# A hybrid decoder block on one core: pads that put TensorE's operands at multiples of 512 bytes, one weight cast behind q's evictions, and other filler amounts around the attention values

## The chip, the cores and the metric

The kernel runs on one core of one Trainium2 chip. The metric is the device time of one execution in microseconds (us); several runs give a median. The profile is of one further execution. Engines are named as in the profile: PE is TensorE's matmul, PEld its weight load, DVE is VectorE, ACT is ScalarE, POOL is GpSimd, and SP is the queue from which most DMAs are issued.

## The reference

One decoder layer for 512 tokens of width 1024, in float32.

```python
h = rmsnorm(x, g_mix)
q_r,k_r,v_r,g_r, q_f,k_f,v_f,f_f, a_r,a_f = split(h @ w_in)
y_r = (silu(g_r) * groupnorm(retention(rot(q_r), rot(k_r), v_r))) @ w_ret_o   # 4 heads
y_f = forgetting_attention(rmsnorm(q_f), rmsnorm(k_f), v_f, log_sigmoid(f_f + b)) @ w_fox_o   # 8 heads of 64
x = x + (sigmoid(a_r) * y_r + sigmoid(a_f) * y_f) @ w_out
h2 = rmsnorm(x, g_ffn)
x = x + (silu(h2 @ w_gate) * (h2 @ w_up)) @ w_down                             # inner width 2816
```

Forgetting attention is causal softmax attention whose scores get the difference of two cumulated log forget gates added.

## The kernel before, in words

**Products.** Every float32 operand is split into a high and a low part (`wh`, `wl` for weights, `xh`, `xl`, `orh`, `orl`, `ofh`, `ofl`, `mgh`, `mgl`, `xfh`, `xfl` for activations, `hl` for both halves of the hidden activations and `ps` for both parts of the feed-forward weights). A product is three matmuls (`three`: high by high, low by high, high by low) into one PSUM bank. Most matmuls stream 512 columns of float32 against 128 x 128 stationary values. A weight unit of 128 x 1024 goes through four steps: a DMA on SP's queue into `raw` (`load_w`, through `move`, L69), ACT's cast into `wh` and DVE's difference into `wl` (`split_raw`, L160), and PE's matmuls. A unit takes a `raw` buffer (2) and a `wh`/`wl` buffer (3), so loads run ahead of PE by a few units.

**Order of the work.** After a start of some 5 us PE runs: the first token products (to about 66 us), q of the attention branch in two cuts of 256 and 264 columns (66 to 97 us), k and v (to 149 us), and then the gates. All of these are generators in one `Fill` (L281): `fill(x)` advances it by x us of PE work as the code reckons it (3 matmuls of 512 columns count 0.64, L28). Between the fills stand the steps of retention and of the attention ("fox"). So the amounts handed to `fill` set the order on PE. `pinned` keeps PE's, and `moves` SP's, instructions in the order in which the code issues them.

**q.** `tok_group` (L257) runs the cuts one after another; a cut uses four PSUM banks, one for each 128 tokens, and the second cut begins in the banks of the first, when `evac_qf` (L643) has copied them out with ACT. q has four weight units: 0 and 1 for the first cut, 2 and 3 for the second.

**Attention.** The loop (L947 to L972) makes 32 score steps: 4 pairs of heads `a`, 2 heads `e` in a pair, 4 query blocks `i`. A step makes two matmuls, then DVE's minimum and ACT's exponential; two steps later DVE transposes `pr` into `psq`. The transposed probabilities of a head are turned across partitions through DRAM: `fox_put` (L757) writes `psq` to `pd`, `fox_get` (L772) reads it back as `pT` in four DMAs that wait until the write has landed. Both go through SP's queue, in the order of the code, with the loads of weights (`raw`), forget-gate rows (`cb`) and row scales (`rd`, `rw`) between them. Pair `a`'s values (`fox_values`, L784; 16 matmuls `pT,vf`, called V0 to V3 here) stand at step 8(a+2)+1, behind `fill(VF)`. After a score step `fill(SF[i])` runs, where i counts down 3, 2, 1, 0; behind the last score steps `fill(TAIL)`.

**The stages after that.** The gate products and y_r (`orh`) to 285 us, W_fo (`ofh`) to 310 us, W_out (`mgh`, `mgl`) to 354 us, the feed-forward's gate and up products (`gu`, `ps,xfh`) to 568 us, and the down product (`hl,ps`) from 569 us. The parts `ps` go round a ring of three buffers r0, r1, r2, where r2 lies in the pool `fq`; `hl` lies in three other places, one of them (`b2f`) in `fq` too.

**Addresses.** [...] Three pads fill up what small tiles leave: `PAD_CST` (L108) ahead of the weight pool, `PAD_SM` (L109) on the right side, `PAD_FTOK` (L919) in the token pool. Distances of the first byte from the last multiple of 512, in the built program:

| tiles that PE reads | before |
|---|---|
| wh, wl, later mgh, mgl, and the pool fq (r2, b2f) | 32 |
| xh, xl, orh, orl, ofh, ofl, xfh, xfl, the ring's r0 and r1, the other two places of hl | 192 |
| retention's and the attention's working tiles | 448 |

So a product `xh,wh` streams or holds an operand that begins 32 bytes past a multiple of 64 and another that begins on a multiple of 64; `mgh,wh` has both at 32, and `ps,xfh` has both at 192, or one at 32 where ps is in r2.

Of the kernel before, what the change touches and what calls it, by code (L numbers as in the profile page):

```python
# [13 lines left out]
AF = mybir.ActivationFunctionType  # L14
# [13 lines left out]
MM3 = 3 / 2400.0  # L28
WARM = 8 * (512,) + 3 * (128,)
NEG = -1e30  # L30
PAD_CST, PAD_FTOK, PAD_SM = 107, 104, 16

C_GMIX = 0
C_GFFN = C_GMIX + NK
# [17 lines left out]
def block_kernel(ctx: ExitStack, tc, x, xT, c_early, c_tab, c_late, w_qf, w_tok, w_vg, w_a, w_y, w_o, w_gu, w_gl, w_dn, w_dh, out):  # L52
# [3 lines left out]
    act = nc.scalar.activation  # L56
    pinned = [False, None]

    def after(ins, prev):

        tc.add_manual_dep(ins.ins, prev.ins.name, mybir.DependencyInfo(mybir.DependencyClass.NoSync, mybir.DependencyReason.DATA), reason="order")
# [38 lines left out]
    def bank(tag):  # L100
        return ps.tile([P, 512], F32, name=tag, tag=tag, bufs={"acc": 4, "sc": 2, "tp": 2}[tag])
# [39 lines left out]

    WU, WP = 1056, 1152
    RAW, WB, SG, PT, CBUF, LEAD = 2, 3, 16, 2, 3, 2
    RF, CF, PF, SF, LAG = (5.72, 4.64, 6.8, 4.2, 11.2, 4.4), (3.0, 2.0, 2.26, 4.0), 5.9, (0.63, 0.83, 1.57, 1.4), 2
    VF, TAIL = 1.8, 2.6

    raw_pools, part_pools, turns = [wp] * RAW, [wp] * WB, [0, 0]

# [19 lines left out]
    def split_w(src, width=1024):  # L168
        h, l = ready.pop(0) if ready else split_raw(begun.pop(0) if begun else load_w(src, width), width)
        due[0] = LEAD  # L170
        return h, l
# [9 lines left out]
    def three(o, sh, sl, mh, ml, first, last):  # L181
        due[0] -= 1
        if due[0] == 0 and coming:
            begun.append(load_w(*coming.pop(0)))
        mm(o, lhsT=sh, rhs=mh, start=first, stop=False)
        mm(o, lhsT=sh, rhs=ml, start=False, stop=False)
        mm(o, lhsT=sl, rhs=mh, start=False, stop=last)
# [14 lines left out]
    for k in range(NK):  # L202
        u, cs = k // 2, slice(k % 2 * 512, k % 2 * 512 + 512)
# [53 lines left out]
    def tok_group(src, evac, cuts=(512,), done=(), behind=None):  # L257

        u = 0
        for c, w in enumerate(cuts):  # L260
            accs = [bank("acc") for _ in range(NT)]
            kpu = 1024 // (w // 256 * 256)
            for k in range(NK):
                if k % kpu == 0:
                    h, l = done[u] if u < len(done) else split_w(src(u, w * kpu), w * kpu)
                    if behind is not None and u == len(done):
                        after(split_raw.last[0], behind)
                    u += 1
                cs = slice(k % kpu * w, k % kpu * w + w)
                for t in range(NT):  # L270
                    tq = slice(t * P, (t + 1) * P)
                    three(accs[t][:, :w], xh[:, k, tq], xl[:, k, tq], h[:, cs], l[:, cs], k == 0, k == NK - 1)
                    if k == NK - 1:
                        evac(t, c, accs[t])
                    yield w * MM3
# [226 lines left out]
    fox = {}  # L502
# [107 lines left out]
    qf = ftok.tile([P, NT, FH * FD], F32, name="qf", tag="qf")  # L610
# [31 lines left out]

    def evac_qf(t, c, acc):  # L643
        sc = rstd1[:, t:t + 1]
        act(out=qf[:, t, c * 256:c * 256 + 256], in_=acc[:, 0:256], func=AF.Copy, scale=sc)  # L645
        if c:
            fox["fz"] = stt(out=fz[:, t, :], in0=acc[:, 256:264], scalar=sc, in1=ce[:, C_BF:C_BF + FH], op0=ALU.mult, op1=ALU.add)
            if t == NT - 1:
                for u in range(NT):
                    qnorm(u)  # L650
# [188 lines left out]
    def y_ret(mp):  # L839

        def evac(m2, acc):
# [4 lines left out]

    pinned[0] = True
    fill = Fill(tok_group(lambda u, width: w_qf[u, :, :width], evac_qf, (256, 264), (queue_q,), turn_act[0]),
                tok_group(unit(1), evac_kf), tok_group(unit(0), evac_to(vf, AF.Copy)), gates(0), gates(1), gates(2), gates(3), *(y_ret(mp) for mp in range(4)))
    coming += [(w_qf[u, :, :w * 4], w * 4) for u, w in ((1, 256), (2, 264), (3, 264))] + [(w_tok[g, u], 1024) for g in (1, 0) for u in range(4)]  # L850
    coming += [(w_a[g, mp, u], 1024) for mp in range(4) for g in range(2) for u in range(2)] + [(w_y[g, mp], 1024) for g in range(2) for mp in range(4)]
# [569 lines left out]
    def u_tile():  # L1421
        turns_u[0] += 1
        return u2[:, turns_u[0] % 2]

    turns_u = [0]
    for g in range(4):
# [12 lines left out]
        u = u_tile()  # L1439
# [131 lines left out]
```

## Time and profile before

| | |
|---|---|
| median of 3 runs | 692.83 us (692.82 to 693.55) |
| the profiled execution | 692.4 us, of it 690.6 span |
| PE busy | 682.4 us (99%), 3375 matmuls |
| PEld busy | 562.3 us (81%) |
| DVE busy | 536.1 us (78%) |
| ACT busy | 362.3 us (52%) |
| POOL busy | 53.5 us (8%) |
| DMA | 100.51 MB, mean 146 GB/s |
| granted TensorE clock | 1.000 |
| chain that ended last | PE 64%, DMA 3%, DVE 1%, ACT 1% |

The span runs from the first to the last instruction; the 1.8 us around it are in the time of an execution and not in the profile. The times of a row are a start, a duration, an engine, a line, an operation and the tiles `out<-in`, with a count; a bracket holds the idle time ahead of it and what ended that. A matmul's duration overlaps with that of the next, so PE's pace is read from the distance of starts and not from durations.

### The profile page before, as it was taken

The numbers are of one execution on the slowest core, as the hardware profiler recorded it, in microseconds if no ns is written. First come the engines' busy times: TensorE is split into PE (matmuls) and PEld (weight loads), VectorE is DVE, ScalarE is ACT, GpSimd is POOL, SyncE is SP. The second block draws the span as 40 slices with busy tenths as digits, with TensorE's granted clock in tenths as the row PEclk, the third lists the DMA queues.
The fourth block names the chain that finished last, engine by engine and source line by source line (L and its number), as shares of the span: only waits on it lengthen the run. The fifth ranks groups of instructions, "written<-read, shape, count | busy, mean of one in ns | idle before, by whom it ended". The sixth has DMA issues, their size and how long they took to land.

```text
span 690.6 us, 9419 instructions
## 1 busy us (share of the span) xinstructions
PE 682.4 (99%) x3375; PEld 562.3 (81%) x3375; DVE 536.1 (78%) x878; ACT 362.3 (52%) x551; POOL 53.5 (8%) x73
## 2 busy tenths in 40 slices
PE   9999999999999999999999999999999999999998
PEld 6887988887787768788888888888888898888997
DVE  6899458966688655496988898989889887756794
ACT  6777354642455435354576655564646474443341
POOL 0033600000122210000130000000000000000000
PEclk9999999999999999999999999999999999999999
DMA  8900543624648878527611516545362523654221
GB/s 290 398 7 31 134 158 93 214 92 153 198 136 264 235 193 247 166 92 263 224 62 45 200 30 166 136 140 154 86 177 59 143 72 62 158 144 156 80 103 62
DMA packets 85806, 100.51 MB, mean 146 GB/s; under 512 B 52960, under 2 KB 62464, under 8 KB 84992
## 3 DMA queue, kind: packets, MB, share of 16 engines
q1 hardware_dynamic: 84976, 98.86, 46.3%
q10 hardware_dynamic: 784, 1.07, 0.6%
q8 instruction: 26, 0.43, 0.3%
q14 instruction: 20, 0.16, 0.1%
HBM read 82.50 MB, written 10.58 MB: 135 GB/s over the span
## 4 chain that ended last, share of the span: by engine, by line
PE 64%; DMA 3%; DVE 1%; ACT 1%; SPq 0%; issue 0%; DVEq 0%; ACTq 0%
PE acc L81 49%; PE sc L81 11%; PE tp L81 4%; DMA pT<-pd 1%; DMA pd<-psq 1%; DMA tk<-tk 1%; SPq L71 0%; ACT ps L1073 0%; DVE ps L1074 0%; DVE b L1082 0%; ACT us L1236 0%; DVE us L1286 0%; DVE hl L1130 0%; DVE us L1235 0%; DVE pf L1460 0%
## 5 line engine op out<-in xcount | busy, mean ns | idle before, releaser
L81 PE MATMUL acc<-ps,xfh 128*128 128x512 f32 (+1 forms) x576 | 168.3, 374 | 0.3 <-ACT us L1195 0.3
L81 PEld LDWEIGHTS acc<-ps,xfh 128*128 128x128 f32 x576 | 105.3, 188 | 21.0 <-ACT us L1195 0.5
L1073 ACT CAST ps<-b 128x1024 fp32r<-128x1024 f32 (+1 forms) x84 | 82.2, 979 | 61.3 <-PE acc L81 27.4
L1074 DVE TENSOR_TENSOR ps<-b,ps 128x1024 fp32r<-128x1024 f32 (+1 forms) x84 | 94.4, 1135 | 22.2 <-ACT ps L1073 21.0
L81 PE MATMUL acc<-ps,xfl 128*128 128x512 f32 (+1 forms) x288 | 107.9, 375 | 0.0
L164 ACT CAST wh<-raw 128x1024 fp32r<-128x1024 f32 (+1 forms) x44 | 46.0, 1048 | 90.9 <-PE acc L81 50.5
L165 DVE TENSOR_TENSOR wl<-raw,wh 128x1024 fp32r<-128x1024 f32 (+1 forms) x44 | 55.0, 1251 | 36.4 <-ACT wh L164 36.4
L81 PEld LDWEIGHTS acc<-ps,xfl 128*128 128x128 f32 x288 | 54.2, 188 | 10.0
L1082 DVE TENSOR_TENSOR b<-b,b 128x1024 f32<-128x1024 f32 (+1 forms) x48 | 52.1, 1124 | 0.0
L81 PE MATMUL acc<-wh,xh 128*128 128x512 f32 (+2 forms) x144 | 50.4, 350 | 1.1 <-ACT qf L645 1.1
L81 PE MATMUL acc<-xh,wh 128*128 128x512 f32 x128 | 51.3, 401 | 0.0
L81 PE MATMUL acc<-xl,wh 128*128 128x512 f32 x128 | 50.7, 396 | 0.0
L81 PE MATMUL acc<-xh,wl 128*128 128x512 f32 x128 | 50.7, 396 | 0.0
L81 PE MATMUL acc<-wh,xl 128*128 128x512 f32 (+2 forms) x144 | 49.9, 347 | 0.0
L81 PE MATMUL acc<-wl,xh 128*128 128x512 f32 (+2 forms) x144 | 49.5, 344 | 0.0
L81 PE MATMUL acc<-hl,ps 128*128 128x512 f32 x168 | 40.9, 392 | 0.0
L81 PEld LDWEIGHTS acc<-hl,ps 128*128 128x128 f32 x168 | 31.6, 188 | 7.1
L1195 ACT COPY us<-acc 128x512 f32<-128x512 f32 (+1 forms) x48 | 26.2, 551 | 17.6 <-PE acc L81 16.6
L1121 DVE TENSOR_TENSOR ps<-raw,ps 128x1024 fp32r<-128x1024 f32 x14 | 17.1, 1221 | 19.7 <-ACT ps L1118 19.7
L81 PEld LDWEIGHTS acc<-wh,xh 128*128 128x128 f32 x144 | 27.1, 188 | 5.3 <-ACT qf L645 1.3
L743 ACT ACTIVATE pr<-pr,nm 128x512 f32<-128x512 f32 (+3 forms) x32 | 18.0, 563 | 23.6 <-DVE nm L741 23.3
L81 PEld LDWEIGHTS acc<-wl,xh 128*128 128x128 f32 x144 | 27.2, 189 | 3.6
(296 smaller groups left out, 1437.6 us busy)
## 6 DMA issues: line engine op xcount, KB each, us to landing
b<-in_w_gu_dram SPq DMA_DIRECT2D x40, 512.0 KB, 4.6
raw<-in_w_a_dram SPq DMA_DIRECT2D x16, 512.0 KB, 5.5
raw<-in_w_dn_dram SPq DMA_DIRECT2D x14, 512.0 KB, 4.0
pd<-psq SPq DMA_DIRECT2D x8, 640.0 KB, 6.5
pT<-pd SPq DMA_DIRECT2D x32, 160.0 KB, 3.5
pf<-squares SPq DMA_DIRECT2D x160, 32.0 KB, 2.0
blk<-in_w_vg_dram SPq DMA_DIRECT2D x8, 512.0 KB, 10.5
raw<-in_w_tok_dram SPq DMA_DIRECT2D x8, 512.0 KB, 4.6
```

Source lines behind the costliest of these rows:

```text
L81: in_order(nc.tensor.matmul(o, **kw))
L164: split_raw.last = (nc.scalar.copy(out=h[:, :width], in_=raw[:, :width]), tt(out=l[:, :width], in0=raw[:, :width], in1=f32(h)[:, :width], ...
L165: tt(out=l[:, :width], in0=raw[:, :width], in1=f32(h)[:, :width], op=ALU.subtract))
L743: fox["last"] = act(out=pr[:, :n], in_=pr[:, :n], func=AF.Exp, scale=-1.0, bias=nm, accum_out=fox["rs", a][:, e, i:i + 1])
L1073: part.cast = nc.scalar.copy(out=h, in_=raw)
L1074: low = tt(out=l, in0=raw, in1=f32(h), op=ALU.subtract)
L1082: queue(tt(out=raws[g][b][v], in0=raws[g][b][v], in1=raws[g][c][v], op=ALU.add))
L1121: tt(out=l, in0=raw, in1=f32(h), op=ALU.subtract)
L1195: copy = nc.scalar.copy(out=u_(tp, slot), in_=os[tp][:, :w])
```

## The change

```diff
-PAD_CST, PAD_FTOK, PAD_SM = 107, 104, 16
+PAD_CST, PAD_FTOK, PAD_SM = 99, 128, 64
...
-    RF, CF, PF, SF, LAG = (5.72, 4.64, 6.8, 4.2, 11.2, 4.4), (3.0, 2.0, 2.26, 4.0), 5.9, (0.63, 0.83, 1.57, 1.4), 2
-    VF, TAIL = 1.8, 2.6
+    RF, CF, PF, SF, LAG = (5.72, 4.64, 6.8, 4.2, 11.2, 4.4), (3.0, 2.0, 2.26, 4.0), 5.9, (0.5, 0.7, 1.45, 1.3), 2
+    VF, TAIL = 2.8, 2.6
...
                     if behind is not None and u == len(done):
                         after(split_raw.last[0], behind)
+                    if u == 3 and c:
+                        after(split_raw.last[0], fox["qe"])
                     u += 1
...
     def evac_qf(t, c, acc):
         sc = rstd1[:, t:t + 1]
-        act(out=qf[:, t, c * 256:c * 256 + 256], in_=acc[:, 0:256], func=AF.Copy, scale=sc)
+        fox["qe"] = act(out=qf[:, t, c * 256:c * 256 + 256], in_=acc[:, 0:256], func=AF.Copy, scale=sc)
```

**Pads.** In the built program after, all tiles of the table above begin at a multiple of 512. The number of instructions and their sizes stay.

**Cast.** The high-part cast of q's fourth weight unit gets an order dependency on the last eviction of q's first cut. On ACT's queue, before, around the four evictions (`qf<-acc`, 128x256); `wh<-raw 128x1056` are the casts of q's third and fourth unit, `rK<-rT` a copy for retention:

```order
L475 ACTIVATE gs<-gs,rstd_86 128x512 x3
L164 CAST wh<-raw 128x1024
L164 CAST wh<-raw 128x1056 x2
L537 COPY rK<-rT 128x512
L645 ACTIVATE qf<-acc,rstd_86 128x256 x4
L164 CAST wh<-raw 128x1024
L537 COPY rK<-rT 128x512
```

The same place of ACT's queue after; line numbers behind L267 are larger by 2:

```order
L477 ACTIVATE gs<-gs,rstd_86 128x512 x3
L164 CAST wh<-raw 128x1024
L164 CAST wh<-raw 128x1056
L539 COPY rK<-rT 128x512
L647 ACTIVATE qf<-acc,rstd_86 128x256 x4
L164 CAST wh<-raw 128x1056
L164 CAST wh<-raw 128x1024
L539 COPY rK<-rT 128x512
```

One 1056-wide cast has moved from ahead of the copy and the four evictions to behind them.

**Filler amounts.** The four amounts behind score steps fall by 0.13, 0.13, 0.12 and 0.1, and the amount ahead of the values rises from 1.8 to 2.8. In filler products (three matmuls each) on PE from the first score step: V0 stands behind 55 before and 53 after, V1 behind 72 and 70, V2 behind 90 and 89, V3 behind 125 and 126. Between the 8th score step and V0 stand 20 before and 19 after, between the 16th and V1 23 and 24, between the 24th and V2 24 and 26.

The loads of weights are issued when a filler begins a new unit, so they move against the puts in SP's queue. SP's queue before, from the first read-back (`pT<-pd`) on; `pd<-psq` is a head's put and `raw<-in_w_a_dram` a weight unit of the gates:

```order
L71 DMA pT<-pd 32x4x320 x4
L71 DMA raw<-in_w_a_dram 128x1024
L71 DMA pd<-psq 128x1280
L71 DMA cb<-cd 128x512
L71 DMA rd<-rt 128x32
L71 DMA pT<-pd 32x4x320 x4
L71 DMA rw<-rd 64x4x128 x2
L71 DMA pd<-psq 128x1280
```

The same place of SP's queue after:

```order
L71 DMA pT<-pd 32x4x320 x4
L71 DMA pd<-psq 128x1280
L71 DMA raw<-in_w_a_dram 128x1024
L71 DMA cb<-cd 128x512
L71 DMA rd<-rt 128x32
L71 DMA pT<-pd 32x4x320 x4
L71 DMA rw<-rd 64x4x128 x2
L71 DMA pd<-psq 128x1280
```

The weight load that stood ahead of the put stands behind it. The same happens with the later puts of the stage; SP's queue before, at the third pair's second put, where the first weights of y_r (`in_w_y`) are loaded:

```order
L71 DMA pT<-pd 32x4x320 x4
L71 DMA rw<-rd 64x4x128 x2
L71 DMA raw<-in_w_y_dram 128x1024
L71 DMA pd<-psq 128x1280
L71 DMA raw<-in_w_y_dram 128x1024
L71 DMA pT<-pd 32x4x320 x4
```

That place of SP's queue after:

```order
L71 DMA pT<-pd 32x4x320 x4
L71 DMA rw<-rd 64x4x128 x2
L71 DMA pd<-psq 128x1280
L71 DMA raw<-in_w_y_dram 128x1024 x2
L71 DMA pT<-pd 32x4x320 x4
```

Here the first load of y_r's weights has moved behind the put.

## The prediction

> **What bounds the kernel now.** I read the engines' busy times first, then PE's waits, then the pace of its matmuls.
>
> ```profile
> PE 682.4 (99%) x3375; PEld 562.3 (81%) x3375; DVE 536.1 (78%) x878; ACT 362.3 (52%) x551; POOL 53.5 (8%) x73
> ```
>
> ```profile
> PE tp L81 <- DMA pT<-pd: 1.7, 2, 0.9
> ```
>
> PE is the bound: it is busy for 682.4 of the span's 690.6 us, and the wait that the waits view puts first, on the values' `pT`, is 1.7 us in two. So a gain must come from PE's pace, or from waits of this size.
>
> The pace follows from the distance of starts in one stretch of PE's timeline in the down product. Each part takes 24 matmuls of 512 columns and begins with its `sc` rows:
>
> ```profile
> 596.97 1.56 PE L81 MATMUL sc<-hl,ps 128*128 128x512 f32 x6
> ...
> 602.47 1.55 PE L81 MATMUL sc<-hl,ps 128*128 128x512 f32 x6
> ...
> 613.39 1.57 PE L81 MATMUL sc<-hl,ps 128*128 128x512 f32 x6
> ...
> 619.01 1.57 PE L81 MATMUL sc<-hl,ps 128*128 128x512 f32 x6
> ...
> 624.62 1.55 PE L81 MATMUL sc<-hl,ps 128*128 128x512 f32 x6
> ```
>
> These parts differ only in where hl and ps lie. From 596.97 both begin at 32 past a multiple of 512: 5.50 us, 229 ns a matmul. From 602.47 two parts have both at 192: 10.92 us over 48, 227.5 ns. From 613.39 hl is at 192 and ps at 32: 5.62 over 24, 234.2 ns. From 619.01 hl is at 32 and ps at 192: 5.61, 233.8 ns. So it isn't the one place or the other that costs, nor which of the two operands is streamed; a matmul whose operands begin at different phases of 64 bytes takes 234.0 ns, some 6.5 ns more than one where they agree. After the change all agree. No operand lies at a multiple of 512 before, so that the new phase, 0 with 0, is as fast as 32 with 32 and 192 with 192 is an inference, and I take it because those two agree within 2 ns. Beside it stands a rule of the Trainium skill ("TensorE: Matmul & The Clock Gate", section "Step-by-step: what each phase is for"): streamed and stationary operands come through two independent read ports and the gap is N columns at 2.4 GHz plus 2.5 ns, wherever they lie; the rows above disagree with it by the place and by 12 to 18 ns a matmul.
>
> **Pads.** The matmuls that mix phases, grouped by shape over the whole run:
>
> ```profile
> L81 PE MATMUL acc<-ps,xfh 128*128 128x512 f32 x480 | 150.6, 392 | 0.0
> ```
>
> ```profile
> L81 PE MATMUL acc<-xh,wh 128*128 128x512 f32 x128 | 51.3, 401 | 0.0
> ```
>
> ```profile
> L81 PE MATMUL acc<-hl,ps 128*128 128x512 f32 x168 | 40.9, 392 | 0.0
> L81 PE MATMUL acc<-wh,xh 128*128 128x512 f32 x80 | 32.0, 400 | 0.0
> ```
>
> - Gates: 128 x 3 products = 384, all mixed. y_r and W_fo are written alike, with 4 x 4 x 2 x 3 = 96 each. k and v: 8 x 4 x 3 = 96 each, within the 80 of each product in the last row. Together 768, by 6.5 ns: 5.0 us.
> - Gate and up products: 480 `ps,xfh` and half as many `ps,xfl` in the acc banks, 720, a third of them with ps in r2, which alone mixes: 240 by 6.5 ns, 1.6 us.
> - Down: the acc rows are half of a part, so 168/12 = 14 parts; in 6 of them just one of hl and ps lies in `fq`: 144 by 6.5 ns, 0.9 us.
> - W_out's products and the other two thirds agree already: nothing.
> - The first stage is different:
>
> ```profile
> 5.00:66.00 61.00, 60.27 (x257) 47.95 (x258) 55.58 (x78) 45.53 (x74) 10.09 (x10) 1.00 0.48 181
> 46.00:54.40 8.40, 8.11 (x35) 6.19 (x33) 8.32 (x9) 7.45 (x20) 2.01 (x1) 1.00 0.01 2
> 258.40:310.00 51.60, 51.60 (x227) 40.46 (x226) 32.33 (x43) 24.84 (x35) 0.00 (x0) 1.00 0.54 170
> 370.00:560.00 190.00, 190.00 (x875) 156.99 (x873) 169.92 (x195) 109.27 (x139) 0.00 (x0) 1.00 0.44 122
> ```
>
> After the stretch's bounds and length come the busy times of PE, PEld, DVE, ACT and POOL. 257 matmuls of the first stage mix, 1.7 us by 6.5 ns; but DVE is busy for 8.32 of the 8.40 us ahead of 54.4, so what PE saves before that it waits for there. I take 0.5 (0 to 1.7). Elsewhere PE doesn't wait (51.60 of 51.60, 190.00 of 190.00), and DVE, at 169.92 of 190.00, has room for 1.6 us less there: the cover holds.
>
> Sum of the pads: 5.0 + 1.6 + 0.9 + 0.5 = 8.0 us.
>
> **The cast.** ACT's and PE's timelines at the change from q's first cut to its second:
>
> ```profile
> 78.81 1.07 ACT L164 CAST wh<-raw 128x1056 fp32r<-128x1056 f32 x1 [6.07 <-PE acc L81]
> 79.79 0.61 ACT L537 COPY rK<-rT 128x512 f32<-128x512 f32 x1
> 80.31 1.56 ACT L645 ACTIVATE qf<-acc,rstd 128x256 f32<-128x256 f32 x4
> ```
>
> ```profile
> 80.83 0.39 PE L81 MATMUL acc<-wh,xh 128*128 128x264 f32 x1 [1.05 <-ACT qf L645]
> ```
>
> The cast holds ACT until 79.88 while PE ends the cut at 79.8. Moved behind the evictions, it leaves `rK` and then the first eviction; rK's input must still land, so the eviction comes some 0.4 us sooner, not 1.05: I take 0.4 (0 to 1.0). The cast then begins at about 81.0 rather than 78.81; behind it on ACT stand the next unit's cast and the second rK, behind its `wl` on DVE the raw buffer that SP's next load waits for, and behind that load on SP's queue a transposed read. All of it comes some 2 us later. That unit is the second cut's second half, so PE reaches it only half a cut after 80.83, and I put the harm at 0 (up to 0.5).
>
> **Fillers and SP's queue.** The values of the first and the last pair on PE:
>
> ```profile
> 217.67 1.07 PE L81 MATMUL tp<-pT,vf 128*64 128x512 f32 x2
> 219.57 2.34 PE L81 MATMUL tp<-pT,vf 128*64 128x512 f32 x14 [0.83 <-DMA pT<-pd]
> 221.84 0.50 PE L81 MATMUL acc<-xh,wh 128*128 128x512 f32 x1
> ```
>
> ```profile
> 283.24 2.38 PE L81 MATMUL sc<-pT,vf 128*64 128x512 f32 x16
> 285.54 0.50 PE L81 MATMUL acc<-orh,wh 128*128 128x512 f32 x1
> ```
>
> V3, with everything landed, takes 2.30 us; V0 takes 4.17, since its second head's `pT` isn't there and the two heads run one after another instead of side by side. That is 1.87 us, of which the waits view shows 0.83. The other of the two `pT` waits is V2's and costs alike: 3.7 in all. Where the reads come from, on SP's queue:
>
> ```profile
> 205.03 0.47 SPq L71 DMA_DIRECT2D raw<-in_w_a_dram  x1
> 206.72 0.34 SPq L71 DMA_DIRECT2D pd<-psq  x1
> ...
> 213.19 3.07 SPq L71 DMA_DIRECT2D pT<-pd  x4
> ...
> 217.74 0.60 SPq L71 DMA_DIRECT2D pd<-psq  x1
> 218.80 0.36 SPq L71 DMA_DIRECT2D raw<-in_w_a_dram  x1
> ...
> 222.37 2.69 SPq L71 DMA_DIRECT2D pT<-pd  x4
> ```
>
> The read waits for the put's landing: 6.47 us behind a put that has a weight load just ahead of it, 4.63 behind one whose load stands behind it. After the change the put of 206.72 and the later ones stand ahead of their loads, so V0's second head lands 1.84 sooner. Against this V0 stands 2 fillers earlier, 2 x 3 x 0.234 = 1.4 us, while the scores that feed it move up by about one of these. V0's loss falls from 1.87 to some 0.5 (0 to 3.3). For V2 two more puts of its chain gain such 1.84, and two more fillers stand ahead of it: its loss falls from 1.9 to some 0.7 (0 to 1.9). I take 2.5 gained (from 1.4 lost to 3.7 gained).
>
> The loads pay for it. They go out behind the put, some 1.7 us later by the first two rows. Where that bites is the beginning of y_r, whose first load moves behind a put as well: DVE's and PE's timelines,
>
> ```profile
> 261.32 1.22 DVE L165 TENSOR_TENSOR wl<-raw,wh 128x1024 fp32r<-128x1024 f32 x1 [1.75 <-ACT wh L164]
> ```
>
> ```profile
> 263.23 0.40 PE L81 MATMUL acc<-orh,wl 128*128 128x512 f32 x1
> ```
>
> `wl` ends 0.7 us before PE needs it, so 1.7 us later costs 1.0; since the whole queue also runs ahead, I take 0.5 (0 to 2.0).
>
> **Sum.** 8.0 + 0.4 + 2.5 - 0.5 = 10.4 us less. The profiled execution took 692.4, so 682.0; the median of the runs before, 692.83, is 0.4 above it, so I forecast 682.4.
>
> **The rivals.**
> - *The chain through DRAM sets the stage, and the values wait longer.* If puts and reads land at the same times as before, V0's earlier place only lengthens its wait: the 2.5 is gone, and what the faster fillers save in this stage (about half of the gates' 384 matmuls, 1.3 us) waits too. For it: the 6.47 us of a put with a load ahead may be another transfer's doing. Against: 4.63 with the load behind. Then 692.4 - 10.4 + 2.5 + 1.3 = 685.8, with the 0.4 some 686; with the late load at its dearest, 687.5.
> - *Phases don't matter as such.* PE's pace stays: the Trainium skill has such a rule ("SBUF — State Buffer", section "Who interferes with whom": PE never waits on anyone), and the trace speaks against it. Apart from that rule: the four places in the down product could differ by something that goes with the buffer and not with its address, though I see nothing else that both directions of mixing share. Then only q, the queue and the late load are left: 692.4 - 0.4 - 2.5 + 0.5 = 690.0, with the 0.4 some 690.4.
> - *Slower: at a multiple of 512 the stream and the stationary values meet in the same place, and a matmul with both there runs like a mixed one.* Place: every product of 512 columns that agreed before, 480 of `ps,xfh` and `ps,xfl` and 192 of `hl,ps`. Price: 672 x 6.5 ns = 4.4 us lost and nothing of the pads gained, and values that wait as before: 696.8, with the 0.4 some 697. It decides when the pace at 0 with 0 is above the mean of today's, (1152 x 234.0 + 672 x 227.5) / 1824 = 231.6 ns. Against it: the two agreeing phases that the trace has are both the fast ones.
> - *Faster still: the new phase is better than any now.* No row shows it; every ns below 227.5 is worth some 1.8 us by the same 1824 matmuls, so 224 would give 676.
>
> **How the numbers follow.** A measurement of this kernel tells about 0.2%, 1.4 us, from no change. My forecast has a chance of 0.64, the values' waits 0.18, no effect of phases 0.09, the slower one 0.04, faster still 0.05. The forecast's own range: 678 with the first stage's 1.2, all of the values' 3.7 and no late load's 0.5, 0.6 for q, 0.3 for the sc banks left out above and 0.6 for a third of a ns of pace; 686 with the waits of the first rival. The second end goes to 687.5 for that rival at its dearest. So 678 to 687.5; outside are the no-effect, slower and most of the faster-still cases, 0.16. Faster by over 0.2%: 0.64 + 0.18 + 0.05 and half of the no-effect case's 0.09, with its 690.4 a little below the bound 691.4, some 0.92; within 0.2%: 0.04; slower: 0.04.
>
> **What would show it.** After: no stretch of 512-column matmuls at 234 ns; 24 matmuls of every part of the down product in 5.46 us, and the gates' fillers at 0.68 instead of 0.70 us. The first `acc` of q's second cut with a wait of about 0.6. V0 and V2 under 3.1 us each, with their puts landed in 4.6 to 5.8 us. DVE still short of full before 568 us. The forecast is wrong if products with both operands at multiples of 512 run above 230 ns, if the values take 4 us or more as before, or if `orh,wl` waits more than 2 us at its first weights.

## The result, and the profile after

| | before | after |
|---|---|---|
| median, runs of one chip | 693.19 us (692.82 to 695.34, 4 runs) | 681.85 us (680.91 to 682.66, 4 runs) |
| ratio | | 0.983, 95% interval 0.9805 to 0.9854 |
| the profiled execution | 692.4 us, span 690.6 | 681.54 us, span 679.8 |

The change is faster by 1.7%; forecast were 682.4 us within 678 to 687.5. The profiled executions differ by 10.9 us, the working gave 10.4.

PE is still the bound, with 10.4 us less of busy time for the same 3375 matmuls:

```profile
PE 672.0 (99%) x3375; PEld 561.7 (83%) x3375; DVE 537.1 (79%) x878; ACT 361.8 (53%) x551; POOL 57.5 (8%) x73
```

The down product's parts after, from the timeline of PE; 24 matmuls lie between one `sc` row and the next:

```profile
597.73 1.52 PE L81 MATMUL sc<-hl,ps 128*128 128x512 f32 x6
...
603.17 1.52 PE L81 MATMUL sc<-hl,ps 128*128 128x512 f32 x6
...
608.62 1.52 PE L81 MATMUL sc<-hl,ps 128*128 128x512 f32 x6
```

Here "mixed" are matmuls whose two operands begin at different distances past a multiple of 512, and "agreeing" those whose operands begin at the same distance. Every part from 570.53 on takes 5.44 or 5.45 us, 226.7 ns a matmul; none takes the 5.6 us that mixed parts took. PE's five largest waits after:

```profile
PE tp L81 <- DVE warm L111: 1.2, 1, 1.2
PE tp L81 <- DVE ofl L805: 0.9, 1, 0.9
PE acc L81 <- ACT qf L647: 0.7, 1, 0.7
PE sc L81 <- DVE wl L219: 0.7, 1, 0.7
PE acc L81 <- DVE wl L165: 0.5, 1, 0.5
```

The wait on `pT` is gone as a row of its own, and a wait of a score on DVE's `ofl` has come. The values on PE after:

```profile
213.18 3.16 PE L81 MATMUL tp<-pT,vf 128*64 128x512 f32 x16
216.27 0.50 PE L81 MATMUL acc<-xh,wh 128*128 128x512 f32 x1
...
231.83 3.52 PE L81 MATMUL sc<-pT,vf 128*64 128x512 f32 x16
235.29 0.50 PE L81 MATMUL acc<-xh,wh 128*128 128x512 f32 x1
...
250.29 2.37 PE L81 MATMUL tp<-pT,vf 128*64 128x512 f32 x16
252.59 0.50 PE L81 MATMUL acc<-xh,wh 128*128 128x512 f32 x1
```

V0 takes 3.09 us, V1 3.46, V2 2.30. Against an undisturbed 2.30 the three lose 2.0 us. Before, V0 lost 1.9, and V1 and V2 looked like this:

```profile
236.51 3.13 PE L81 MATMUL sc<-pT,vf 128*64 128x512 f32 x16
239.57 0.51 PE L81 MATMUL acc<-xh,wh 128*128 128x512 f32 x1
...
254.25 1.07 PE L81 MATMUL tp<-pT,vf 128*64 128x512 f32 x2
256.17 2.34 PE L81 MATMUL tp<-pT,vf 128*64 128x512 f32 x14 [0.86 <-DMA pT<-pd]
258.44 0.51 PE L81 MATMUL acc<-xh,wh 128*128 128x512 f32 x1
```

V1 took 3.06 us and V2 4.19, so the three lost 4.5 us.

Where the time went, by the moment at which the same matmul starts in both traces:

| stage | saved, us | forecast |
|---|---|---|
| first products, to 62 us | 0.1 | 0.5 |
| q's change of cut, 80.83 to 80.42 | 0.3 | 0.4 |
| to the first score, 188.52 to 185.91 | 2.2 | pace |
| first score to the first `orh`, 74.2 to 71.6 us long | 2.7 | pace, values, late load |
| y_r and W_fo, to the first `mgh` | 1.4 | pace |
| W_out | 0.1 | 0 |
| gate and up products | 2.9 | 1.6 |
| down product, `hl,ps` | 1.3 | 0.9 |
| from there to the end | -0.1 | 0 |

### The profile page after: what moved, and what is told of

Its sections match the earlier page's. It is cut to its first block, busy times and chain, and to the rows that moved or that the text cites. A ratio compares the mean times of both kernels' runs of the same rounds, so it can differ in the third digit from the quotient of the medians.

```text
span 679.8 us, 9417 instructions
## 1 busy us (share of the span) xinstructions
PE 672.0 (99%) x3375; PEld 561.7 (83%) x3375; DVE 537.1 (79%) x878; ACT 361.8 (53%) x551; POOL 57.5 (8%) x73
## 4 chain that ended last, share of the span: by engine, by line
PE 88%; DVE 4%; DMA 3%; ACT 2%; issue 1%; SPq 0%; POOL 0%; DVEq 0%; ACTq 0%; POOLq 0%
PE acc L81 68%; PE sc L81 14%; PE tp L81 6%; DMA raw<-in_w_tok_dram 1%; DMA rT<-zr 1%; DVE wl L165 1%; DMA pd<-psq 1%; DVE ps L1076 1%; ACT wh L164 1%; ACT ps L1075 1%; DMA b<-in_w_gl_dram 0%; ACT rz L311 0%; DVE blk L411 0%; DVE psq L757 0%; DVE gs L483 0%
## 5 line engine op out<-in xcount | busy, mean ns | idle before, releaser
L81 PEld LDWEIGHTS acc<-wh,xl 128*128 128x128 f32 x144 | 27.2, 189 | 3.2
```

The lines of the kernel that those rows point to most:

```text
L81: in_order(nc.tensor.matmul(o, **kw))
```

## The experiments

Each kernel's time and ratio stand beside runs of the kernel before on the same chip. Intervals of ratios are 0.3 to 0.6% wide, so that differences of under some 2 us between kernels are not read from medians. What a trace shows of such a difference is one execution, and that varies too: e9, whose order in the attention's stage is that of after, took 73.0 us from the first score to the first `orh`, where after took 71.6.

**e1_pads: the pads alone.**

```diff
-PAD_CST, PAD_FTOK, PAD_SM = 107, 104, 16
+PAD_CST, PAD_FTOK, PAD_SM = 99, 128, 64
```

> The kernel before with the three new pads alone; order and fillers as before. Theory (terms add up, pace by phase): every 512-column matmul at 227 ns; the pads' part of the trace after, about 9 us of the 10.9 saved, comes here, so some 684 beside 693; V0 and V2 lose as much as before, 1.9 us each. Rival (the DRAM chain of the attention sets that stage, so the pace gained there is waited away): the first score to the first y_r product takes as long as before, 74.2 us, and the time is some 685.5 to 686.

Measured: 685.73 us, ratio 0.9874 (0.9855 to 0.9893). The pace is 227 ns everywhere, but the rival was right about the attention. From the first score to the first `orh` it took 75.5 us, 1.2 more than before, though the fillers are faster. V0, V1 and V2 on its PE:

```profile
214.45 1.07 PE L81 MATMUL tp<-pT,vf 128*64 128x512 f32 x2
216.94 2.34 PE L81 MATMUL tp<-pT,vf 128*64 128x512 f32 x14 [1.42 <-DMA pT<-pd]
219.21 0.50 PE L81 MATMUL acc<-xh,wh 128*128 128x512 f32 x1
...
233.67 1.07 PE L81 MATMUL sc<-pT,vf 128*64 128x512 f32 x2
235.39 2.34 PE L81 MATMUL sc<-pT,vf 128*64 128x512 f32 x14 [0.64 <-DMA pT<-pd]
237.66 0.50 PE L81 MATMUL acc<-xh,wh 128*128 128x512 f32 x1
...
252.49 1.07 PE L81 MATMUL tp<-pT,vf 128*64 128x512 f32 x2
254.84 2.34 PE L81 MATMUL tp<-pT,vf 128*64 128x512 f32 x14 [1.28 <-DMA pT<-pd]
257.11 0.50 PE L81 MATMUL acc<-xh,wh 128*128 128x512 f32 x1
```

They take 4.76, 3.99 and 4.62 us: 6.5 lost instead of 4.5. Faster fillers reach the values sooner, the puts land as late as before (6.0 to 7.4 us for seven of the eight), so the stage gives its pace back as waits. The time is the rival's 685.5 to 686, not the theory's 684.

**e2_order: cast and fillers alone**, the kernel after with the old pads.

```diff
-PAD_CST, PAD_FTOK, PAD_SM = 99, 128, 64
+PAD_CST, PAD_FTOK, PAD_SM = 107, 104, 16
```

> The kernel after with the old pads: cast and fillers alone. Theory: mixed phases keep 234 ns; q's wait falls by 0.3 us, V0 and V2 lose some 1 us each less or more, and the new wait of 1 us on DVE's ofl stays, so 1.5 to 2 us less, some 691. Rival (the shorter values come from the pads, the order alone gives nothing): puts land in 6 to 7 us as before, V0 and V2 take 4 us, and the time is that of before.

Measured: 692.48 us, ratio 0.9969 (0.9953 to 0.9985): the theory's 1.5 to 2 us, within its interval. The two ratios multiply to 0.9843, about that of the whole. V0, V1 and V2 take 4.31, 3.89 and 2.31 us: V2 loses nothing any more, but V0's 4.3 is what the rival said. The profiled execution was the longest of its eight (694.81 us). It has a longer wait at q, which e9 takes up, and a granted clock of 0.5 from 83.2 to 86.7 us; its stage from the first score to the first `orh` took 74.8 us, no less than before. So the 0.3% stands on the medians, and this trace doesn't show where it was won.

**e3_both32 and e4_diff64: does the phase within 64 bytes decide?** One pad of the kernel before, in e3 and in e4. The pads count in units of four bytes; the tiles at 32 before lie on the side that the expectations call left, those at 192 on the right.

```diff
-PAD_CST, PAD_FTOK, PAD_SM = 107, 104, 16
+PAD_CST, PAD_FTOK, PAD_SM = 107, 104, 24
```

> The kernel before with PAD_SM 24 instead of 16 and nothing else: the right side's tiles move from 192 to 160 past a multiple of 512, so that left (32) and right (160) have the same phase of 32 bytes past a multiple of 64; none lies on a multiple of 64. Theory (agreement of the phase counts, not the phase): 227 ns, some 684 as with the three pads. Rival (starting on a multiple of 64, 128 or 512 counts): 234 ns everywhere, ps,xfh and hl,ps that ran at 227 now too, 4 us and more on top of before, some 697.

```diff
-PAD_CST, PAD_FTOK, PAD_SM = 107, 104, 16
+PAD_CST, PAD_FTOK, PAD_SM = 131, 104, 16
```

> The kernel before with PAD_CST 131 instead of 107 and nothing else: the left side's tiles move from 32 to 128, the right side's stay at 192, so both start on multiples of 64 but are 64 bytes apart by 128 and by 512. Theory (agreement by 64 bytes is all): 227 ns, some 684. Rival (operands must agree by 128, or lie at multiples of 512): 234 ns for the mixed ones as before, some 693.

Measured: e3 691.79 us, ratio 0.9963 (0.995 to 0.9977); e4 692.1 us, 0.9966 (0.9947 to 0.9986). Neither theory nor rival: a third of a per cent, where the theory wanted over one. The down product in e3, with a part whose operands both begin at 160 and then one with 160 and 32, 128 bytes apart:

```profile
607.33 1.52 PE L81 MATMUL sc<-hl,ps 128*128 128x512 f32 x6
...
612.77 1.56 PE L81 MATMUL sc<-hl,ps 128*128 128x512 f32 x6
...
618.36 1.56 PE L81 MATMUL sc<-hl,ps 128*128 128x512 f32 x6
```

5.44 us and 5.59: 226.7 ns against 232.9. In e4, first hl at 192 against ps at 128, then hl at 128 against ps at 192, 64 bytes apart:

```profile
614.07 1.53 PE L81 MATMUL sc<-hl,ps 128*128 128x512 f32 x6
...
619.56 1.56 PE L81 MATMUL sc<-hl,ps 128*128 128x512 f32 x6
...
625.16 1.54 PE L81 MATMUL sc<-hl,ps 128*128 128x512 f32 x6
```

5.49 and 5.60 us: 228.8 and 233.3 ns, the streamed `hl` being the higher of the two in the first and the lower in the second. Operands of one phase within 64 bytes still pay, so that phase isn't the rule.

**e5_all32 and e6_diff256: which agreement is it?**

```diff
-PAD_CST, PAD_FTOK, PAD_SM = 107, 104, 16
+PAD_CST, PAD_FTOK, PAD_SM = 107, 128, 56
```

> The kernel before with pads 107, 128, 56: all the tiles that the change puts at multiples of 512 begin 32 bytes past one. Theory (streamed and stationary operands must have the same place within 512 bytes, whichever it is): 227 ns everywhere, the time of the three new pads alone, some 686. Rival (it must be a multiple of 512 or at least of 64): 232 to 234 ns everywhere, 4 us on top of before, some 697.

```diff
-PAD_CST, PAD_FTOK, PAD_SM = 107, 104, 16
+PAD_CST, PAD_FTOK, PAD_SM = 83, 104, 16
```

> The kernel before with PAD_CST 83: left tiles at 448, right tiles at 192 past a multiple of 512, 256 apart. Theory (they must agree within 512): mixed products stay at 229 to 234 ns as they did 64 and 128 bytes apart, some 691 to 693. Rival (agreement within 256 is enough): 227 ns, some 686.

Measured: e5 686.13 us, ratio 0.9896 (0.9865 to 0.9927); e6 686.16 us, 0.9892 (0.9864 to 0.992): both as the new pads alone. The down product in e5, all at 32:

```profile
607.64 1.52 PE L81 MATMUL sc<-hl,ps 128*128 128x512 f32 x6
...
613.08 1.52 PE L81 MATMUL sc<-hl,ps 128*128 128x512 f32 x6
```

and in e6, where this part has hl at 192 and ps at 448:

```profile
607.22 1.52 PE L81 MATMUL sc<-hl,ps 128*128 128x512 f32 x6
...
612.66 1.52 PE L81 MATMUL sc<-hl,ps 128*128 128x512 f32 x6
```

5.44 us in both. So it isn't the place: 32, 160, 192 and 0 past a multiple of 512 run alike. It is the distance between streamed and stationary operand: 0 and 256 bytes give 226.7 ns, 64, 128 and 160 give 229 to 234. The theory said within 512; its rival, within 256, is what the runs show for these distances. Others, under 64 bytes above all, weren't tried.

**e7_vf_old and e8_sf_old: which filler amount matters?** The kernel after, with one amount set back in each:

```diff
-    VF, TAIL = 2.8, 2.6
+    VF, TAIL = 1.8, 2.6
```

> The kernel after with VF back at 1.8: V0, V1, V2 behind 52, 67 and 84 fillers instead of 53, 70 and 89; the puts stay ahead of the loads. Theory (the chain through DRAM sets when the values can run, fillers ahead of them only cover it): V1 and V2 lose 1 to 2 us more each, V0 0.5 more, so 2 to 4 us more than after, 684 to 686. Rival (the puts' place in the queue is what paid, the amount ahead of the values nothing): within 1 us of after, 682.

```diff
-(0.5, 0.7, 1.45, 1.3)
+(0.63, 0.83, 1.57, 1.4)
```

> The kernel after with SF back at 0.63, 0.83, 1.57, 1.4: V0, V1, V2 behind 56, 75 and 95 fillers, and weight loads ahead of most puts again. Theory (a load ahead of a put makes it land 1 to 2 us later, but 3 to 6 fillers more, 2 to 4 us, cover that): puts land in 6 to 7 us, the values lose 0 to 2 us in all as in after, so within 1 us of 682. Rival (the puts' place decides): V0 to V2 lose 4 us or more as in the pads alone, some 684 to 686.

Measured: e7 686.62 us, ratio 0.9901 (0.987 to 0.9932); e8 682.43 us, 0.9834 (0.9802 to 0.9866). In e7, V1 on PE:

```profile
231.18 1.07 PE L81 MATMUL sc<-pT,vf 128*64 128x512 f32 x2
234.99 4.50 PE L81 MATMUL sc<-pT,vf 128*64 128x512 f32 x14 [2.74 <-DMA pT<-pd]
239.42 0.80 PE L81 MATMUL acc<-xh,wh 128*128 128x512 f32 x1
```

V1 takes 8.24 us, V0 4.24 and V2 2.30, although the puts that feed them stand ahead of their loads as in after. Not all of V1's time is the wait. From its first matmul to the one that the read held up pass 3.81 us; then 14 matmuls take 4.50 us where e1's take 2.34, because PE's granted clock had fallen. The window from 234.3 to 241.0 us, with the granted clock as the third number from the end:

```profile
234.30:241.00 6.70, 6.01 (x18) 3.62 (x19) 3.90 (x10) 2.12 (x6) 1.17 (x3) 0.50 0.68 238
```

The half clock made that execution, the longest of its four, some 3.0 us longer (2.2 in V1, 0.8 in the five matmuls behind it). The run with a clock of 1.000 took 685.61 us, within the theory's 684 to 686. What the wait grew by against after is half V1's place and half the landing: counted from the first score, V1 began 1.3 us sooner than in after, and its last read landed 1.3 us later. So the larger amount ahead of the values is worth some 4 us (685.61 against after's 681.85), but how much of it is cover and how much a late landing, one trace doesn't show; V2, which the theory had as a loser too, lost nothing.

In e8 three to six fillers more stand ahead of the values; the stage takes 71.8 us beside after's 71.6, though V0 and V1 there take 4.17 and 3.75 us, 3.3 lost where the theory had 0 to 2. So the smaller amounts behind scores add nothing to the larger amount ahead of the values that these runs can tell. The rival on the puts' place isn't tested by e8: only the first two of its eight puts have a weight load issued right ahead, not most of them, as the expectation had it.

**e9_no_cast: the cast's own part.** The kernel after without

```diff
-                    if u == 3 and c:
-                        after(split_raw.last[0], fox["qe"])
```

> The kernel after without the moved cast; pads and fillers as after. Theory (rK's copy, ahead of the evictions on ACT, waits for its DMA rT, which lands as late as the cast ended; so the moved cast frees nothing): the first matmul of q's second cut waits 0.8 to 1.3 us, and the time is that of after, 682, within 0.3. Rival (the cast was worth its 0.3 to 0.4 us): some 682.3, with waits above those of after by that much.

Measured: 683.4 us, ratio 0.9856 (0.9831 to 0.988), which overlaps with that of after. The wait at q was 1.11 us in e9; over all profiled executions it was 0.84 to 1.33 with the cast ahead of the evictions (before, e1, e3 to e6, e9) and 0.41 to 1.63 with the cast behind (after, e2, e7, e8, e10 to e12). So the two groups overlap. Why, ACT in e2 shows, whose wait was longest:

```profile
80.20 0.62 ACT L539 COPY rK<-rT 128x512 f32<-128x512 f32 x1 [7.62 <-DMA rT<-zr]
80.72 1.56 ACT L647 ACTIVATE qf<-acc,rstd 128x256 f32<-128x256 f32 x4
```

The copy that stands between the cut's end and the evictions now waits for its own DMA. There that takes the cast's place; whether the cast is worth anything stays open at the size of 0.3 us.

**e10_vf36: more of the same.** The kernel after with

```diff
-    VF, TAIL = 2.8, 2.6
+    VF, TAIL = 3.6, 2.6
```

> The kernel after with VF 3.6 instead of 2.8: V0, V1, V2 behind 55, 72 and 92 fillers instead of 53, 70 and 89, puts and loads in nearly the same order. Theory (what V0 and V1 still lose, 0.8 and 1.2 us, and the 1.1 us of a score behind V0, is short cover): two fillers, 1.4 us, more ahead of each close most of it; 1 to 2.5 us less than after, some 680. Rival (a later V pushes its DVE work and the next puts back as far, so the chain keeps its distance): V1 and V2 lose 1 us or more each, and the time is 682 or above.

Measured: 684.38 us, ratio 0.9857 (0.9837 to 0.9877). The values lose only 0.6 us, as the theory had it, and yet the stage takes 73.7 us, 2.1 more than after. SP's queue in it:

```profile
224.49 0.38 SPq L71 DMA_DIRECT2D raw<-in_w_a_dram  x1
224.91 0.43 SPq L71 DMA_DIRECT2D pd<-psq  x1
...
232.71 1.27 SPq L71 DMA_DIRECT2D pT<-pd  x3
```

More fillers ahead of the values reach the next weight unit sooner, so its load has moved ahead of the put again, and the read comes 7.80 us behind the put. And PE's waits have others in them:

```profile
PE acc L81 <- DVE wl L165: 1.9, 2, 1.4
...
PE acc L81 <- ACT wh L164: 0.8, 1, 0.8
```

The fillers themselves waited for weights (1.4 on `wl`, 0.8 on `wh`, at 228 to 231 us). Behind these waits the granted clock fell to a half here too, from 231.5 to 234.9 us:

```profile
231.60:234.90 3.30, 3.30 (x10) 2.70 (x9) 1.95 (x8) 2.20 (x7) 0.92 (x2) 0.50 0.57 173
```

The fillers' matmuls then start 430 ns apart (232.04, 232.47, 232.90), which costs some 1.6 us. So of the stage's 2.1 us most follows: the waits for weights put the fillers back by 2.5 us and this stretch by 1.6, while the values lose 1.4 less than in after and no score waits on `ofl`, 1.1 less; that leaves 1.6. The time is the rival's 682 or above, but not for its reason, and neither theory nor rival named the weights or the clock. The two runs of e10 whose clock was 1.000 took 683.00 and 683.79 us, still above after's median.

**e11_early_scores: scores closer together, fillers kept for the values.**

```diff
-(0.5, 0.7, 1.45, 1.3)
+(0.4, 0.6, 1.4, 1.25)
-    VF, TAIL = 2.8, 2.6
+    VF, TAIL = 4.2, 2.6
```

> The kernel after with SF 0.4, 0.6, 1.4, 1.25 and VF 4.2: scores closer together, V0, V1, V2 behind 54, 71 and 92 fillers of which 7, 6 and 12 stand right ahead of the values. Theory (distance from the scores to the values is what counts): V0 to V2 lose under 1 us in all, some 680. Rival (scores that follow each other closer wait for DVE, ACT and their banks, which are what feeds the puts): new waits of 0.5 us and more at score matmuls, and 682 or above.

Measured: 680.63 us, ratio 0.9812 (0.9791 to 0.9833). V0 to V2 on PE:

```profile
214.14 2.37 PE L81 MATMUL tp<-pT,vf 128*64 128x512 f32 x16
216.45 0.50 PE L81 MATMUL acc<-xh,wh 128*128 128x512 f32 x1
...
232.46 2.37 PE L81 MATMUL sc<-pT,vf 128*64 128x512 f32 x16
234.76 0.50 PE L81 MATMUL acc<-xh,wh 128*128 128x512 f32 x1
```

Each takes 2.30 us, V2 too: nothing is lost, as the theory said, and the stage takes 70.0 us. The rival's new wait is there too, 1.4 us of a score on DVE's `ofl`:

```profile
217.81 0.70 DVE L796 TENSOR_TENSOR tp<-tp,rw 128x512 f32<-128x512 f32 x1 [0.38 <-DMA rw<-rd]
220.62 1.10 DVE L757 STREAM_TRANSPOSE psq<-pr 128x256 f32<-128x256 f32 x3 [2.11 <-DMA pd<-psq]
221.64 0.65 DVE L805 TENSOR_TENSOR ofl<-tp,ofh 128x512 fp32r<-128x512 f32 x1
```

DVE stands for 2.11 us at transposes that need a buffer which a put is still reading, and behind them stands the last reader of the bank that the next score needs.

**e12_ofl_first:** e11 with `ofl` ahead of the transpose that the code issues next.

```diff
-                nc.vector.transpose(out=to[:, c:c + (k1 - k0) * step + 1:step], in_=squares_[:, k0:k1 + 1])
+                turned = nc.vector.transpose(out=to[:, c:c + (k1 - k0) * step + 1:step], in_=squares_[:, k0:k1 + 1])
+                if fox.get("ofl") is not None:
+                    after(turned, fox.pop("ofl"))
...
-        tt(out=l, in0=o, in1=f32(h), op=ALU.subtract)
+        fox["ofl"] = tt(out=l, in0=o, in1=f32(h), op=ALU.subtract)
```

> The kernel of e11 with one order more on DVE: the next head's transposes into psq, which wait for an earlier put to land, come behind the low part of the values' output instead of ahead of it. Theory (DVE's queue holds the bank that the next score needs, since the transpose ahead waits for the put): the wait on DVE's ofl, 1.4 us in e11, falls under 0.4 and the time is 0.5 to 1.3 us below e11, some 679.5. Rival (the transposes behind it then feed the next put late): the next values lose that time instead, and the time is that of e11, 680.6.

Measured: 680.42 us, ratio 0.9807 (0.979 to 0.9824). The edit didn't do what it was to do: it moved the 128-wide last transpose of the head before, and the three waiting ones still stand ahead of `ofl`, where they waited 0.93 us. The stage took 69.0 us, 1.0 less than in e11, and the wait on `ofl` isn't in PE's list; the earlier landing of that put goes with it, and one profile can't tell whether the edit or the run made it so. e11 and e12 have the lowest medians of the study, 1.2 to 1.4 us below after; their intervals overlap with its own, so that they aren't shown to be faster.

## Why the prediction was right, and where its steps weren't

- **PE's pace bounds it, and agreement makes it fast.** Right: the pace is 226.7 ns with the operands at multiples of 512, and the waits alone (e2) give 0.3%. The rivals that phases don't matter, or that meeting at a multiple of 512 slows PE, are out. The Trainium skill's rule of independent read ports and N columns at 2.4 GHz plus 2.5 ns ("TensorE: Matmul & The Clock Gate", section "Step-by-step: what each phase is for") has no term for where the operands lie, and would have put e3 to e6 at one pace; they differ by up to 7 ns with the distance of the addresses alone. What the second rival takes from the Trainium skill, that PE never waits on anyone, is about engines that share ports; these runs move only PE's own two operands and don't test it.
- **The step "a matmul whose operands begin at different phases of 64 bytes" was wrong**, without harm to the sum. The four cases of before couldn't tell 64 from 256 bytes, since its only distances were 0 and 160. e3 and e4 show that one phase of 64 bytes isn't enough, e6 that one phase of 256 is. The pads chosen put every such operand at a multiple of 512, which satisfies both rules, so the forecast didn't hang on which of them holds.
- **The pads' sum** was 8.0 us. The gate and up products gave 2.9 instead of 1.6 and the down product 1.3 instead of 0.9. The prediction counted only the mixed parts in the `acc` banks, at 6.5 ns a matmul. By the starts of single matmuls in the two traces, of the 2.9 us these gave 1.8, the mixed ones in the `sc` bank 0.4, and the agreeing ones 0.8. The agreeing parts' means of 227.5 to 229 ns, from which the 6.5 was worked out, aren't a pace of their own: the 229 from 596.97 on is 224 to 236 ns for the first nine of its 24 matmuls and 226.7 for all but the last of the others. The same is seen in the gate and up products, behind every change of the operands' places: the first eight matmuls are slow, also where the next operands agree, and the rest run at 226.7. So the gain is 7.3 ns a mixed matmul and the slow beginnings besides. Why a change of place slows the next ones stays open.
- **First stage:** 0.1 of the 0.5. DVE is still busy for 8.31 of the 8.40 us ahead of 54.4; what PE saves it waits for there (0.53 us on `wl` at 54.55, where before it waited 0.35 at 54.46).
- **The cast:** the forecast's 0.4 and the trace's 0.3 agree by chance. The prediction named the input that must still land; e2's row shows that the wait for it can take all of the gain.
- **The values:** 2.5 forecast, 2.6 found against before, in part by luck: V0 gained 1.1 instead of 1.4, V2 1.9 instead of 1.2, and V1, which the prediction leaves out, lost 0.4 more. Yet the first rival, waits that take the place of the pace, holds for the pads alone (e1); the order's worth beside the pads is the 3.9 us between a stage of 75.5 and one of 71.6, or 2.5 by e9's 73.0. And the reason given was but half of it: puts ahead of their loads do land sooner (5.2, 4.3, 5.7 and 4.5 us for the second to the fifth put after, where before they took 6.4, 4.6, 6.6 and 7.3), but e7 keeps these places and loses the gain, so the amount ahead of the values is needed too. The counts of filler products given with the change hold in their differences; from the first score matmul V0 to V3 stand behind 33, 50, 68 and 103 before and 31, 48, 67 and 104 after.
- **y_r's late load:** 0.5 forecast, none found; `orh,wl` waits for nothing in after. In its stead a score starts 1.1 us late, since it waits for its bank behind DVE's `ofl`, which the prediction didn't name (0.9 us of it in the waits view). These two misses and those of the pads lie on both sides of zero, so that 10.4 forecast against 10.9 found is closer than the terms are.

## What to carry to other kernels

Where PE is the bound, compare starts of like matmuls that differ only in which buffer they read: here three pads, changed by 32 to 192 bytes a partition, were worth 1.2%, as soon as streamed and stationary operands lay a multiple of 256 bytes apart. A faster filler in front of a chain through DRAM turns into a wait unless its amount is raised with it, and one queue that serves both must be read again after each such step, since amounts also move loads past puts. Waits that end on a DMA differ by half a microsecond and more from run to run, so an edit of that size isn't shown by one profile. And read the granted clock of the stretch before a long matmul is put down to its operands or a longer stage to its waits (e7, e10).

## What the runs showed of the hardware

- 512-column matmuls of this kernel's kind start every 226.7 ns when the operands lie 0 or 256 bytes apart by 512 (e5, e6, after), 233 ns at 128 apart (e3), 229 at 64 apart with the streamed operand higher and 233 with the stationary one higher (e4), and 234 at 160 apart (before).
- In before, the first nine matmuls from 596.97 on took 224 to 236 ns, though that part agrees and so do the parts on both sides of it: both operands had moved from 192 to 32. The rest took 226.7. In e3, where they move by 128 bytes instead of 160, the same part had one slow matmul (231 ns), and in after, e5 and e6, where nothing or 256 bytes lies between the places, it had none.
- In three profiles PE's granted clock fell to 0.5 in the midst of its work, for 3.4 us (e2 from 83.2, e10 from 231.5) or 6.8 us (e7 from 234.2). It began during a wait of PE of 2.7 us (e7), 2.0 us after one of 1.6 us (e2) and 1.0 us after two of 0.8 and 1.4 us (e10). Two waits of 1.7 us in e5 were not followed by it.
- The DMA from `psq` to `pd`, 640 KB, took 3.9 to 8.5 us from issue to landing over the 14 profiles: a median of 7.1 us for the 49 puts with a weight load of 512 KB issued right ahead of them (4.9 to 8.5), and 5.1 us for the 63 others (3.9 to 7.3).
